# Reading 32-bit matmul operands from two places in turns: a hybrid DeltaNet and block-attention layer on one Trainium2 core

## The chip, the core and the metric

The kernel runs on one core of a Trainium2 chip. A core has five engines that run side by side and meet at semaphores: TensorE (PE) for matmuls, ScalarE (ACT) and VectorE (DVE) for elementwise work, GpSimd (POOL), and SyncE (SP), which here issues the transfers from memory. TensorE holds one operand of a matmul in its array (the stationary one, brought there by a weight load) and streams the other one through it column by column (the moving one). Matmul results go to PSUM, which has eight banks; all else lies in SBUF.

The metric is device time in microseconds (us) of one execution, and of several runs the median is taken.

## What is computed

One decoder layer for 256 tokens of width 1024. A normalised and modulated input goes through one wide projection. Its columns feed a gated DeltaNet branch (4 heads of 128, chunks of 64 tokens) and a block attention branch (8 heads of 64); both come back to width 1024, are gated and summed, go through an output projection, and are added to the input.

```python
h = rms_norm(x, g_pre) * (1 + scale[:, None, :]) + shift[:, None, :]
qkv_dn, z_dn, beta_logit, a_logit, qkv_mb, z_mb, merge_logit = jnp.split(h @ w_in, cuts, axis=-1)
qkv_dn = jax.nn.silu(causal_depthwise_conv(qkv_dn, conv_w))
o_dn = gated_delta_rule_chunked(l2_normalize(q_dn), l2_normalize(k_dn), v_dn, g, beta)
o_dn = rms_norm(o_dn.transpose(0, 2, 1, 3), dn_norm_g) * jax.nn.silu(z_dn...)
y_dn = o_dn.reshape(b, s, DN_WIDTH) @ w_proj_dn
o_mb = moba_attention(q_mb, k_mb, v_mb)[:, :, :s]
y_mb = (o_mb.transpose(0, 2, 1, 3).reshape(b, s, MB_WIDTH) * jax.nn.silu(z_mb)) @ w_proj_mb
gate_dn, gate_mb = jnp.split(jax.nn.sigmoid(merge_logit), N_BRANCH, axis=-1)
mixed = (gate_dn * y_dn + gate_mb * y_mb) @ w_out
return x + gate[:, None, :] * rms_norm(mixed, g_post)
```

With 256 tokens there is one attention block, so the attention is plain causal attention over 256 keys.

## The kernel before

All tensors are float32. A large product is made of three matmuls in the type float32r, a rounded 32-bit form that goes through TensorE in one pass: each operand is split into a rounded part `hi` and a rest `lo`, and hi·hi, lo·hi and hi·lo are summed in PSUM. For a weight this split is one ACT instruction (`CAST whi<-raw`) and one DVE instruction (`wlo<-raw,whi`) for each 512 KB tile (`split`). Small products, with plain float32 operands, take four passes, and the trace has two records for each of them. Transposes are also done by TensorE.

The stages, with the names that the trace shows:

- **start, x**: x is loaded, its row norms are computed, and 16 float32 matmuls with a diagonal matrix transpose and scale it into `xT`.
- **first** (`ada`, `h_ops`, `phase1`): eight steps k. Each loads two 512 KB tiles of the modulation weights (`wss`), which DVE reduces, and two of the input weights (`raw`); ACT and DVE make `hhi[k]` and `hlo[k]` from `xT`; then 48 float32r matmuls of 256 columns add into eight PSUM banks. Weights are stationary there, `hhi` and `hlo` are moving.
- **conv, norm, decay, gram, subst, quad, rec**: the DeltaNet chain, mostly short DVE steps and small float32 matmuls, ending in a square root over `so`, the normalised output `AT<-bank_d,so`, eight transposes (`bank_d<-pr,AT`) and the split of the result into `obh`, `obl` (`o_out`).
- **att**: scores, softmax and values of four pairs of heads; results in `obh`, `obl` too.
- **gemm**: 16 jobs, the other columns of the wide projection. Fifteen have 48 float32r matmuls of 256 columns; job 6 (`gemm_v`) has 48 of 264 columns. In jobs 6 and 7 `hhi` and `hlo` are stationary and the weights are moving. They have no hurry, so they stand between the small steps of the two branches as work for TensorE.
- **proj, out, tail**: 8 times 24 float32r matmuls of 256 columns from `obh`, `obl` (8 weight tiles `in_wpj`), and the output projection, in each of 8 steps 3 x 3 matmuls of 512 and 3 x 2 of 256 columns (8 weight tiles `in_wo`); then the final norm and the store.

The order on each engine is decided at build time by `Machine.schedule`. Every call through `T`, `A`, `V`, `G` or `DQ` only records an instruction; each instruction has a price (`price`) and a rank (the longest priced path behind it), to which `BOOST`, a table of numbers by stage, is added. A list scheduler then picks, engine by engine, the ready instruction with the highest sum. On the chip the order on each engine is fixed. An engine that waits for one instruction holds up all that is queued behind it.

Weight tiles go through four `raw` buffers and five pairs `whi`, `wlo`. A load waits until its buffer has been split.

Of the kernel before, what the change touches and what calls it, by code (L numbers as in the profile page):

```python
# [11 lines left out]
AF = mybir.ActivationFunctionType  # L12
# [5 lines left out]
P = 128  # L18
D = 1024
S = 256  # L20
KT = D // P
# [16 lines left out]
class Machine:  # L38
# [13 lines left out]
    BOOST = dict(ada=55100, ada0=3000, ada1=308600, ada3=55200, ada4=-3500, ada5=20900, ada6=-74400, ada7=700, att=300, att0=-800100, att1=-391600, att2=19200, att3=1407600, att4=400, att5=-159100, att6=200900, att7=660900, beta=-4000, conv=635700, conv0=-1113500, conv1=-582700, conv2=-1729900, conv3=198400, conv4=-4800, cut=-634400, cut0=-28600, cut1=162000, cut2=42100, cut5=919400, cut7=-1900, decay=-251800, decay0=4600, decay1=669500, fin0=105600, fin1=-600, first=203500, first0=159700, first2=100, first3=-65100, first4=-89800, first5=105500, first7=-179600, gate=277800, gate0=4300, gate1=38200, gate2=-4400, gate3=13300, gate4=-400, gate5=-48600, gate6=-58900, gate7=284300, gemm=-7900, gemm1=-198800, gemm10=82200, gemm11=535900, gemm12=98200, gemm13=-227200, gemm14=1222400, gemm15=1316400, gemm2=47400, gemm4=61900, gemm5=-847400, gemm6=352100, gemm7=47500, gemm8=-3200, gemm9=-796900, gram=85700, gram0=-275200, gram1=-154600, mod=2100, mod0=-111400, mod1=18700, mod2=-53700, mod3=76700, mod4=-388200, mod5=-7800, mod6=92400, mod7=5500, norm=-269600, norm0=31000, norm1=-11700, norm3=-18200, norm4=80100, norm5=-250700, out0=-818300, out0_0=-46700, out0_1=33900, out0_2=-17900, out0_3=8800, out0_4=1385300, out0_5=27400, out1=-900, out1_0=-6500, out1_2=-16500, out1_3=200, out1_4=-30400, out1_5=-2249400, out1_6=73500, out1_7=4300, prep=-15700, proj=599600, proj1=-200, proj2=-69200, proj3=-361300, proj4=538400, proj5=-6400, proj6=-640500, proj7=-785200, quad=354400, rec=2016500, rest=-200900, start=-187700, subst=100, tail=83100, x=-116200)  # L52
# [71 lines left out]
    def price(part, method, out, ins, args, kw):  # L124
# [123 lines left out]
def block_kernel(ctx: ExitStack, tc: tile.TileContext, I, out):  # L248
# [39 lines left out]

    def tok(t):
        return slice(t * P, (t + 1) * P)  # L290
# [127 lines left out]
    def h_ops(k):  # L418
        hf = mem([P, S], f"hf{k}", tag="cv")
        for h in (hhi[k], hf):  # L420
            A.activation(h, xT[:, k] if k else xb[0][:, 0:S], AF.Identity, bias=ab[:, k, 0:1], scale=ab[:, k, 1:2])
        V.tensor_sub(hlo[k], hf, hhi[k])


    def phase1(k, parts):
        for j in range(16):
# [36 lines left out]
    szd = mem([P, H, S], "szd")  # L463
# [11 lines left out]
    def ev_silu(dst):  # L475
        return lambda b: silus.append(A.activation(dst, v2(b), AF.Silu))

    jobs = [ev_silu(szd[:, 0:2]), ev_silu(szd[:, 2:4]), ev_silu(szm[:, 0:2]), ev_silu(szm[:, 2:4])]
# [13 lines left out]
    lg = mem([P, 2, NT, H], "lg")  # L492

    def gemm_v():

        bs = [bank("g", f"v{t}") for t in range(NT)]
        for k0, k1 in ((0, 3), (3, 6), (6, 8)):
# [4 lines left out]
            for t in range(NT):  # L502
                for k in range(k0, k1):
                    o, c = bs[t][:, 0:VW], slice((k - k0) * VW, (k - k0 + 1) * VW)
                    op = mm(o, hhi[k][:, tok(t)], whi[:, c], k == 0, False)
                    mm(o, hlo[k][:, tok(t)], whi[:, c], False, False)
                    last = mm(o, hhi[k][:, tok(t)], wlo[:, c], False, k == KT - 1)
                    M.behind(op, order[-1:])
                    order.append(last)
        for t in range(NT):  # L510
            V.tensor_copy(lg[:, :, t], bs[t][:, 256:VW].rearrange("p (n h) -> p n h", n=2))
            A.copy(mv[:, t, 0:256], bs[t][:, 0:256])

    def gemm(i):
        b = bank("g", f"g{i}")
        for j in range(2):
            whi, wlo = split(raw("w2", 2 * i + j - 2 * (i > 6)), f"w2{i}{j}")
            for k in range(KT):
                if i == 7:
# [3 lines left out]
                    op = mm(o, h, whi[:, c], kk == 0 and t == 0, False)  # L523
                    mm(o, l, whi[:, c], False, False)
                    last = mm(o, h, wlo[:, c], False, kk == KT - 1)
                else:
                    o = b[:, j * S : (j + 1) * S]
                    op = mm(o, whi[:, tok(k)], hhi[k], j == 0 and k == 0, False)
                    mm(o, whi[:, tok(k)], hlo[k], False, False)
                    last = mm(o, wlo[:, tok(k)], hhi[k], False, k == KT - 1)  # L530
# [41 lines left out]
    M.stage("prep")  # L572

# [52 lines left out]
    def scores(pair):  # L626
# [11 lines left out]
        for h, s_ in banks_.items():  # L638
# [5 lines left out]
            for t, c in cut:  # L644
                ex_ = A.activation(e[:, c], sms[:, c], AF.Exp, bias=mx[:, h, t : t + 1], scale=SCALE, accum_out=rs[:, h, t : t + 1])
# [7 lines left out]
    def values(pair):  # L653
# [21 lines left out]
        A.copy(obh[:, 1, pair], obm)  # L675
        V.tensor_sub(obl[:, 1, pair], obm, obh[:, 1, pair])
# [191 lines left out]
    def o_out(po, t):  # L868
# [196 lines left out]
```

## Time and profile before

| | us |
|---|---|
| median of 3 runs (lowest to highest) | 239.1 (238.16 to 240.05) |
| the profiled execution, its own time | 238.06 |
| its span, from first to last instruction | 236.2 |
| mean granted TensorE clock | 0.988 of full speed |

The profile gives busy time by engine. A matmul's record lasts longer than the distance to the next matmul's start, since matmuls are pipelined; so a busy TensorE says that it has work, and the distance between starts says at what rate it works. The chain of waits follows the work back from the last instruction: a row such as "64.66 28.16 PE bank_g L236 x240" is a stretch that begins at 64.66 us, lasts 28.16 us and consists of 240 records on PE that write bank group g, one after the other with no wait. All instructions are issued from one helper line, L236, so groups are told apart by the tiles that they read and write: "bank_g<-hlo,whi" is a matmul with moving operand hlo and stationary operand whi.

### The profile page before, as it was taken

The numbers are of one execution on the slowest core, as the hardware profiler recorded it, in microseconds if no ns is written. First come the engines' busy times: TensorE is split into PE (matmuls) and PEld (weight loads), VectorE is DVE, ScalarE is ACT, GpSimd is POOL, SyncE is SP. The second block draws the span as 40 slices with busy tenths as digits, with TensorE's granted clock in tenths as the row PEclk, the third lists the DMA queues.
The fourth block names the chain that finished last, engine by engine and source line by source line (L and its number), as shares of the span: only waits on it lengthen the run. The fifth ranks groups of instructions, "written<-read, shape, count | busy, mean of one in ns | idle before, by whom it ended". The sixth has DMA issues, their size and how long they took to land.

```text
span 236.2 us, 4934 instructions
## 1 busy us (share of the span) xinstructions
PE 227.2 (96%) x1902; PEld 216.8 (92%) x1902; DVE 194.9 (83%) x440; ACT 142.1 (60%) x281; POOL 1.2 (1%) x7
## 2 busy tenths in 40 slices
PE   8699999999999999999999999999999999999990
PEld 8699999999999999799998999898999999899980
DVE  0879999987999985689998999699888986488663
ACT  6585565558888675997446563663368841365141
POOL 1000000000000000000000000000000000000000
PEclk9799999999999999999999999999999999999998
DMA  7999999985957767411582410897788630584013
GB/s 219 396 416 406 389 400 337 395 294 181 309 183 276 241 198 205 154 21 72 147 297 81 121 71 0 296 338 253 253 268 298 228 123 0 183 280 162 0 60 120
DMA packets 15271, 51.20 MB, mean 217 GB/s; under 512 B 1680, under 2 KB 2064, under 8 KB 15248
## 3 DMA queue, kind: packets, MB, share of 16 engines
q1 hardware_dynamic: 15248, 50.89, 61.5%
q8 instruction: 15, 0.25, 0.4%
q14 instruction: 8, 0.07, 0.1%
HBM read 49.83 MB, written 1.05 MB: 215 GB/s over the span
## 4 chain that ended last, share of the span: by engine, by line
PE 90%; DMA 4%; DVE 2%; ACT 1%; issue 1%; SPq 0%; DVEq 0%; ACTq 0%
PE bank_g L236 51%; PE bank_d L236 24%; PE bank_m L236 15%; DMA x<-in_x 2%; DMA raw<-in_wo 2%; DVE xT L236 1%; ACT L236 1%; DVE vT L236 1%; ACT DT L236 0%; DVE r L236 0%; SPq L236 0%; DVE AT L236 0%; ACT whi L236 0%; DVEq L1061 0%; DVE so L236 0%
## 5 line engine op out<-in xcount | busy, mean ns | idle before, releaser
L236 ACT CAST whi<-raw 128x1024 fp32r<-128x1024 f32 (+2 forms) x68 | 67.2, 996 | 35.0 <-DMA raw<-in_w 14.7
L236 DVE TENSOR_TENSOR wlo<-raw,whi 128x1024 fp32r<-128x1024 f32 (+2 forms) x68 | 77.6, 1158 | 7.9 <-ACT whi L236 7.0
L236 PE MATMUL bank_g<-hlo,whi 128*128 128x256 f32 x256 | 69.2, 284 | 0.0
L236 PE MATMUL bank_g<-hhi,whi 128*128 128x256 f32 x256 | 69.1, 284 | 0.0
L236 PE MATMUL bank_g<-hhi,wlo 128*128 128x256 f32 x256 | 68.9, 282 | 0.0
L236 PEld LDWEIGHTS bank_g<-hhi,whi 128*128 128x128 f32 x256 | 46.6, 188 | 0.7 <-issue 0.5
L236 PEld LDWEIGHTS bank_g<-hlo,whi 128*128 128x128 f32 x256 | 46.7, 188 | 0.6 <-issue 0.5
L236 PEld LDWEIGHTS bank_g<-hhi,wlo 128*128 128x128 f32 x256 | 46.7, 188 | 0.3 <-issue 0.2
L236 PE MATMUL bank_g<-obl,whi 128*128 128x256 f32 x64 | 13.3, 284 | 0.0
L236 PE MATMUL bank_g<-obh,whi 128*128 128x256 f32 x64 | 13.3, 284 | 0.0
L236 PE MATMUL bank_g<-obh,wlo 128*128 128x256 f32 x64 | 13.2, 283 | 0.0
L236 ACT ACTIVATE hhi<-cv 128x256 fp32r<-128x256 f32 x8 | 3.3, 417 | 13.6 <-DVE cv L236 13.6
L236 ACT ACT_TABLE_LOAD x8 | 10.3, 1283 | 1.7 <-DVE cv L236 0.8
L236 PEld LDWEIGHTS bank_g<-obh,whi 128*128 128x128 f32 x64 | 10.3, 191 | 0.5 <-ACT obh L236 0.2
L236 DVE CUSTOM_DVE_ANT_0 wss<-wss,AT,pr 128x1024 f32<-128x1024 f32 x8 | 10.2, 1280 | 0.3 <-DMA wss<-in_wss 0.3
L236 PEld LDWEIGHTS bank_g<-obh,wlo 128*128 128x128 f32 x64 | 10.3, 191 | 0.2
L236 DVE SCALAR_TENSOR_TENSOR tl<-wss,bank_g 128x512 f32<-128x512 f32 x8 | 5.5, 687 | 5.9 <-PE bank_g L236 5.9
L236 DVE CUSTOM_DVE_ANT_0 wss<-wss,AT,b2g 128x1024 f32<-128x1024 f32 (+1 forms) x8 | 10.2, 1276 | 0.0
L236 PEld LDWEIGHTS bank_g<-obl,whi 128*128 128x128 f32 x64 | 10.1, 191 | 0.1
L236 PE MATMUL bank_g<-whi,hhi 128*128 128x264 f32 (+1 forms) x32 | 9.1, 284 | 0.0
L236 PE MATMUL bank_g<-whi,hlo 128*128 128x264 f32 (+1 forms) x32 | 9.1, 284 | 0.0
L236 PE MATMUL bank_g<-wlo,hhi 128*128 128x264 f32 (+1 forms) x32 | 9.1, 283 | 0.0
(223 smaller groups left out, 448.0 us busy)
## 6 DMA issues: line engine op xcount, KB each, us to landing
raw<-in_w SPq DMA_DIRECT2D x43, 512.0 KB, 4.6
wss<-in_wss SPq DMA_DIRECT2D x15, 512.0 KB, 6.6
raw<-in_wg SPq DMA_DIRECT2D x8, 512.0 KB, 4.7
raw<-in_wpj SPq DMA_DIRECT2D x8, 512.0 KB, 4.3
raw<-in_wo SPq DMA_DIRECT2D x8, 512.0 KB, 4.4
raw<-in_w SPq DMA_DIRECT2D x6, 256.0 KB, 7.3
x<-in_x SPq DMA_DIRECT2D x2, 512.0 KB, 4.1
x<-in_x SPq DMA_DIRECT2D x1, 1024.0 KB, 8.0
```

The lines of the kernel that those rows point to most:

```text
L236: o["ins"] = getattr(self.engines[o["part"]], o["method"])(*o["args"], **o["kw"])
```

## The change

The moving operand of every large float32r matmul is laid out differently, and read in another order.

- **Layout.** Each group of 32 columns of such an operand lies "woven": first the 16 even columns, then the 16 odd ones. The matmul's access pattern (`mmw`) reads from the two halves in turns, so the columns reach the array in their natural order, while the addresses alternate between two places 16 elements apart. Results are written straight to PSUM. For `gemm_v` the whole 264 columns lie as two halves of 132.
- **Who makes the layout.** The weights that are moving (`wo`, `w2[12:14]`, `wv`) are reordered on the host. On the chip, instructions that wrote the operand anyway now read with a stride of two: the copies from PSUM into `xT`, the first `h_ops`, the exponentials of the softmax, the casts and subtractions for `obh`, `obl`.
- **What follows from it.** Where `hhi` and `hlo` are stationary, tokens now come out in woven order; for the values this agrees with the woven softmax, and for the decay logits one `STREAM_SHUFFLE` over 16 columns puts the tokens back. In `o_out` the factor `gd` moves from the DVE multiply into the ACT cast and the DVE subtraction. `szd` has another order of its dimensions.
- **The planner.** The price of a float32r matmul is now `n / 2.4 + 5` ns, the assumed rate of transfers 400 instead of 360, and the table `BOOST` has new numbers throughout.

No matmul, no weight split and no byte of transfer is added or taken away.

```diff
-    BOOST = dict(ada=55100, ada0=3000, ada1=308600,
...
+    BOOST = dict(ada=33200, ada0=-46900, ada1=119400, ada2=-90900,
...
-            held = n * 4 * list(out.ap)[0][1] / 360.0
+            held = n * 4 * list(out.ap)[0][1] / 400.0
...
-                return max(n * 0.4531 + 4, 111.0) - 6 * (list(out.ap)[0][1] < P), 60.0
+                return n / 2.4 + 5, 60.0
...
+    def woven(ap):
+        return ap.rearrange("p (q b a) -> p q a b", b=16, a=2)
+    def lies(ap):
+        return ap.rearrange("p (q a b) -> p q a b", b=16, a=2)
+    def mmw(o, l, r, first, last=True):
+        q = dict(a=2, b=16)
+        return mm(o.rearrange("p (q b a) -> p q b a", **q), l, r.rearrange("p (q a b) -> p q b a", **q), first, last)
...
-    A.copy(xT[:, 1], xb[0][:, S : 2 * S])
+    A.copy(lies(xT[:, 1]), woven(xb[0][:, S : 2 * S]))
     for q in range(1, 4):
-        A.copy(xT[:, 2 * q : 2 * q + 2], v2(xb[q]))
+        A.copy(lies(xT[:, 2 * q : 2 * q + 2].rearrange("p k s -> p (k s)")), woven(xb[q]))
...
-            mm(a, whi[:, c], hhi[k], k == 0 and j % 2 == 0, False)
-            mm(a, whi[:, c], hlo[k], False, False)
-            mm(a, wlo[:, c], hhi[k], False, k == KT - 1)
+            mmw(a, whi[:, c], hhi[k], k == 0 and j % 2 == 0, False)
+            mmw(a, whi[:, c], hlo[k], False, False)
+            mmw(a, wlo[:, c], hhi[k], False, k == KT - 1)
...
+                        rv = r[:, c].rearrange("p (a b) -> p b a", a=2)
+                        last = mm(o.rearrange("p (b a) -> p b a", a=2), l[k][:, tok(t)], rv, k == n == 0, k == KT - 1 and n == 2)
...
-            V.tensor_copy(lg[:, :, t], bs[t][:, 256:VW].rearrange("p (n h) -> p n h", n=2))
+            V.tensor_copy(lgw[:, :, t], bs[t][:, 256:VW].rearrange("p (n h) -> p n h", n=2))
...
+    V.stream_shuffle(lg.rearrange("p n t h -> p (n t h)"), lgw.rearrange("p n t h -> p (n t h)"), [16 * (i % 2) + i // 2 for i in range(32)])
...
-                ex_ = A.activation(e[:, c], sms[:, c], AF.Exp, bias=mx[:, h, t : t + 1], scale=SCALE, accum_out=rs[:, h, t : t + 1])
+                ex_ = A.activation(lies(e[:, c]), woven(sms[:, c]), AF.Exp, bias=mx[:, h, t : t + 1], scale=SCALE, accum_out=rs[:, h, t : t + 1])
...
-        A.copy(obh[:, 1, pair], obm)
-        V.tensor_sub(obl[:, 1, pair], obm, obh[:, 1, pair])
+        A.copy(lies(obh[:, 1, pair]), woven(obm))
+        V.tensor_sub(lies(obl[:, 1, pair]), woven(obm), lies(obh[:, 1, pair]))
...
-        V.scalar_tensor_tensor(ob, v4(pt), pr[:, PSI_GD : PSI_GD + 1], szd[:, :, tok(t)], op0=mul, op1=mul)
-        A.copy(obh[:, 0, :, tok(t)], ob)
-        V.tensor_sub(obl[:, 0, :, tok(t)], ob, obh[:, 0, :, tok(t)])
+        gd = pr[:, PSI_GD : PSI_GD + 1]
+        V.tensor_tensor(lies(ob.rearrange("p h c -> p (h c)")), woven(pt), woven(szd[:, t]), mul)
+        A.activation(obh[:, 0, :, tok(t)], ob, AF.Copy, scale=gd)
+        V.scalar_tensor_tensor(obl[:, 0, :, tok(t)], ob, gd, obh[:, 0, :, tok(t)], op0=mul, op1=sub)
...
+    lie = lambda a: a.reshape(*a.shape[:-1], -1, 16, 2).swapaxes(-1, -2).reshape(a.shape)
+    wo = lie(wo)
+    w2[12:14] = lie(w2[12:14])
+    wv = wv.reshape(P, KT, VW // 2, 2).swapaxes(2, 3).reshape(P, KT * VW)
```

The other calls of `mm` in `gemm`, `out_mm` and `proj` become `mmw` in the same way.

The new table moves instructions on every engine. Two places matter below, both at the end of the DeltaNet chain. The first is ACT around the square root over `so`. Before, it stands there behind the cast of a weight tile (`whi_118<-raw_79`, the first tile of `in_wo`):

```order
L236 ACTIVATE jk_140,so_161<-bank_d_67 128x128
L236 ACTIVATE jk_139,so_161<-bank_d_67 128x128
L236 ACTIVATE wss_75<-bank_g_63 128x512
L236 CAST whi_122<-raw_78 128x1024
L236 ACTIVATE jk_140,so_161<-bank_d_66 128x128
L236 ACTIVATE jk_139,so_161<-bank_d_66 128x128
L236 ACTIVATE jk_140,so_161<-bank_d_66 128x128
L236 ACTIVATE jk_139,so_161<-bank_d_66 128x128
L236 CAST whi_118<-raw_79 128x1024
L236 ACT_TABLE_LOAD
L236 ACTIVATE so_161<-so_161 128x8
L236 ACT_TABLE_LOAD
```

In the changed kernel the same place on ACT has two exponentials of the attention (`pex`) ahead of the square root:

```order
L236 CAST obh_143<-obm_150 128x256
L236 ACTIVATE jk_141,so_162<-bank_d_66 128x128
L236 ACTIVATE jk_140,so_162<-bank_d_66 128x128
L236 ACTIVATE jk_141,so_162<-bank_d_66 128x128
L236 ACTIVATE jk_140,so_162<-bank_d_66 128x128
L236 ACTIVATE pex_89,rs_145<-sms_148,mx_146 128x256
L236 ACTIVATE pex_89,rs_145<-sms_148,mx_146 128x128
L236 ACT_TABLE_LOAD
L236 ACTIVATE so_162<-so_162 128x8
L236 ACT_TABLE_LOAD
L236 ACTIVATE pex_90,rs_145<-sms_149,mx_146 128x256
```

Both casts, of the first `in_wpj` and the first `in_wo` tile, now stand behind the square root, and the attention's last pairs stand where they were.

The second place is PE around the eight transposes (`bank_d<-pr_71,AT_86`) that this square root leads to. Before:

```order
L236 MATMUL bank_g_63<-hhi_0_99,whi_120 128x256
L236 MATMUL bank_g_63<-hlo_0_107,whi_120 128x256
L236 MATMUL bank_g_63<-hhi_0_99,wlo_125 128x256
L236 MATMUL bank_d_65<-pr_71,AT_86 128x128 x4
L236 MATMUL bank_d_67<-pr_71,AT_86 128x128 x4
L236 MATMUL bank_g_63<-hhi_0_100,whi_120 128x256
L236 MATMUL bank_g_63<-hlo_0_108,whi_120 128x256
```

In the changed kernel:

```order
L236 MATMUL bank_g_64<-hhi_0_98,wlo_123 128x256
L236 MATMUL bank_m_69<-pr_71,pex_91 128x128 x3
L236 MATMUL bank_m_70<-pr_71,pex_92 128x128 x3
L236 MATMUL bank_d_65<-pr_71,AT_86 128x128 x4
L236 MATMUL bank_g_64<-hhi_0_99,whi_119 128x256
L236 MATMUL bank_d_67<-pr_71,AT_86 128x128 x4
L236 MATMUL bank_m_69<-pr_71,pex_89 128x128 x3
L236 MATMUL bank_m_70<-pr_71,pex_90 128x128 x3
L236 MATMUL bank_m_68<-sms_147,mv_88 64x256
```

The transposes come earlier among the matmuls of the gemm jobs: 30 of these were left behind them, now 57, and the transposes of two attention pairs stand beside them.

## Rows read from the trace of the kernel before

**Rows 1.** The page's first part: engine, busy us (share of span), instructions.
```profile
PE 227.2 (96%) x1902; PEld 216.8 (92%) x1902; DVE 194.9 (83%) x440; ACT 142.1 (60%) x281; POOL 1.2 (1%) x7
```

**Rows 2.** The span in 40 slices of 5.9 us: granted clock, transfer rate.
```profile
PEclk9799999999999999999999999999999999999998
...
GB/s 219 396 416 406 389 400 337 395 294 181 309 183 276 241 198 205 154 21 72 147 297 81 121 71 0 296 338 253 253 268 298 228 123 0 183 280 162 0 60 120
```

**Rows 3.** The chain of waits: start us, length us, engine, bank, records.
```profile
22.17 0.70 PE bank_d L236 x6
...
57.51 5.63 PE bank_g L236 x46
...
64.66 28.16 PE bank_g L236 x240
...
221.94 6.30 PE bank_d L236 x27
```

**Rows 4.** The chain of waits, small float32 matmuls (gram; state and output).
```profile
123.26 0.86 PE bank_d L236 x4
...
165.42 1.78 PE bank_d L236 x16
```

**Rows 5.** Timeline of PE from 100 us, first and 36th matmul (none missing between).
```profile
99.80 0.28 PE L236 MATMUL bank_g<-hhi,whi 128*128 128x256 f32 x1
...
103.95 0.28 PE L236 MATMUL bank_g<-hhi,wlo 128*128 128x256 f32 x1
```

**Rows 6.** Groups of PE by shape: names, shape, count | busy us, mean ns.
```profile
L236 PE MATMUL bank_g<-hlo,whi 128*128 128x256 f32 x256 | 69.2, 284 | 0.0
...
L236 PE MATMUL bank_g<-obl,whi 128*128 128x256 f32 x64 | 13.3, 284 | 0.0
...
L236 PE MATMUL bank_d<-whi,hlo 128*128 128x512 f32 x24 | 9.0, 396 | 0.0
L236 PE MATMUL bank_m<-hhi,whi 128*128 128x256 f32 x48 | 9.0, 280 | 0.0
...
L236 PE MATMUL bank_g<-whi,hlo 128*128 128x264 f32 x16 | 4.6, 285 | 0.0
...
L236 PE MATMUL bank_d<-xT 128*128 128x256 f32 x16 | 4.1, 379 | 0.0
```

**Rows 7.** Groups of weight loads (PEld) by shape.
```profile
L236 PEld LDWEIGHTS bank_g<-hhi,whi 128*128 128x128 f32 x256 | 46.6, 188 | 0.7 <-issue 0.5
...
L236 PEld LDWEIGHTS bank_d<-vs,ktok 128*128 128x128 f32 x8 | 1.0, 191 | 0.0
```

**Rows 8.** Busy us by engine in stretches of 10 us: PE, PEld, DVE, ACT, POOL.
```profile
30.00:40.00 10.00, 10.00 (x88) 10.00 (x87) 10.00 (x14) 5.94 (x9) 0.00 (x0) 1.00 0.99 360
...
60.00:70.00 10.00, 10.00 (x86) 10.00 (x85) 9.97 (x23) 8.64 (x15) 0.00 (x0) 1.00 0.70 236
...
130.00:140.00 10.00, 10.00 (x87) 10.00 (x86) 9.82 (x61) 5.82 (x12) 0.00 (x0) 1.00 0.34 111
```

**Rows 9.** Timeline at the end of the DeltaNet chain: ACT, then PE.
```profile
172.46 1.05 ACT L236 CAST whi<-raw 128x1024 fp32r<-128x1024 f32 x1 [3.59 <-DMA raw<-in_wpj]
...
175.16 1.05 ACT L236 CAST whi<-raw 128x1024 fp32r<-128x1024 f32 x1 [0.61 <-DMA raw<-in_wo]
...
177.52 0.21 ACT L236 ACTIVATE so<-so 128x8 f32<-128x8 f32 x1
...
178.95 1.25 PE L236 MATMUL bank_d<-pr,AT 128*128 128x128 f32 x8 [0.19 <-DVE AT L236]
```

**Rows 10.** Groups of DVE and ACT by shape, nearest to the touched instructions.
```profile
L236 DVE SCALAR_TENSOR_TENSOR bt<-bank_d,pr,szd 128x512 f32<-128x512 f32 x2 | 1.5, 751 | 0.3 <-PE bank_d L236 0.2
...
L236 DVE TENSOR_TENSOR obl<-bt,obh 128x512 fp32r<-128x512 f32 x2 | 1.4, 684 | 0.0
...
L236 DVE STREAM_SHUFFLE cv<-jk 128x88 f32<-128x88 f32 x1 | 0.3, 252 | 0.0
...
L236 ACT ACTIVATE pex<-sms,mx 128x256 f32<-128x256 f32 x8 | 4.0, 506 | 2.2 <-DVE mx L236 2.2
```

More of the change, by code (lines that the diff above doesn't have):

```diff
@@ L420, in h_ops @@
         for h in (hhi[k], hf):
-            A.activation(h, xT[:, k] if k else xb[0][:, 0:S], AF.Identity, bias=ab[:, k, 0:1], scale=ab[:, k, 1:2])
+            A.activation(lies(h), lies(xT[:, k]) if k else woven(xb[0][:, 0:S]), AF.Identity, bias=ab[:, k, 0:1], scale=ab[:, k, 1:2])
         V.tensor_sub(hlo[k], hf, hhi[k])
@@ L462, in block_kernel @@
     mv = mem([P, NT, 512], "mv", tag="mv")
-    szd = mem([P, H, S], "szd")
+    szd = mem([P, NT, H * P], "szd")
     szm = mem([P, H, S], "szm")
@@ L492, in block_kernel @@
     lg = mem([P, 2, NT, H], "lg")
+    lgw = mem([P, 2, NT, H], "lgw")
     def gemm_v():
@@ L504, in gemm_v @@
                     o, c = bs[t][:, 0:VW], slice((k - k0) * VW, (k - k0 + 1) * VW)
-                    op = mm(o, hhi[k][:, tok(t)], whi[:, c], k == 0, False)
-                    mm(o, hlo[k][:, tok(t)], whi[:, c], False, False)
-                    last = mm(o, hhi[k][:, tok(t)], wlo[:, c], False, k == KT - 1)
+                    turns = [(hhi, whi), (hlo, whi), (hhi, wlo)]
+                    for n, (l, r) in enumerate(turns):
+                        rv = r[:, c].rearrange("p (a b) -> p b a", a=2)
+                        last = mm(o.rearrange("p (b a) -> p b a", a=2), l[k][:, tok(t)], rv, k == n == 0, k == KT - 1 and n == 2)
+                        op = op if n else last
                     M.behind(op, order[-1:])
@@ L522, in gemm @@
                     o, h, l = b[:, t * 256 : (t + 1) * 256], hhi[kk][:, tok(t)], hlo[kk][:, tok(t)]
-                    op = mm(o, h, whi[:, c], kk == 0 and t == 0, False)
-                    mm(o, l, whi[:, c], False, False)
-                    last = mm(o, h, wlo[:, c], False, kk == KT - 1)
+                    op = mmw(o, h, whi[:, c], kk == 0 and t == 0, False)
+                    mmw(o, l, whi[:, c], False, False)
+                    last = mmw(o, h, wlo[:, c], False, kk == KT - 1)
                 else:
                     o = b[:, j * S : (j + 1) * S]
-                    op = mm(o, whi[:, tok(k)], hhi[k], j == 0 and k == 0, False)
-                    mm(o, whi[:, tok(k)], hlo[k], False, False)
-                    last = mm(o, wlo[:, tok(k)], hhi[k], False, k == KT - 1)
+                    op = mmw(o, whi[:, tok(k)], hhi[k], j == 0 and k == 0, False)
+                    mmw(o, whi[:, tok(k)], hlo[k], False, False)
+                    last = mmw(o, wlo[:, tok(k)], hhi[k], False, k == KT - 1)
                 M.behind(op, order[-1:])
@@ L935, in out_mm @@
         o = outs[n][:, 0 : c1 - c0]
-        mm(o, mh[m][:, tok(t)], whi[:, c0:c1], m == 0, False)
-        mm(o, ml[m][:, tok(t)], whi[:, c0:c1], False, False)
-        mm(o, mh[m][:, tok(t)], wlo[:, c0:c1], False, m == 7)
+        mmw(o, mh[m][:, tok(t)], whi[:, c0:c1], m == 0, False)
+        mmw(o, ml[m][:, tok(t)], whi[:, c0:c1], False, False)
+        mmw(o, mh[m][:, tok(t)], wlo[:, c0:c1], False, m == 7)
         M.stage(*last)
@@ L950, in block_kernel @@
                 c = tok(4 * br + k)
-                mm(o, phi[:, c], obh[:, br, k], br == 0 and k == 0, False)
-                mm(o, phi[:, c], obl[:, br, k], False, False)
-                mm(o, plo[:, c], obh[:, br, k], False, k == 3)
+                mmw(o, phi[:, c], obh[:, br, k], br == 0 and k == 0, False)
+                mmw(o, phi[:, c], obl[:, br, k], False, False)
+                mmw(o, plo[:, c], obh[:, br, k], False, k == 3)
         mt = mem([P, 2, S], f"mt{m}", tag="tl")
```

7 lines of the change are left out of this document (4 added, 3 removed).

## The prediction

> **What bounds the kernel now.** I read the page's engine table first. TensorE is busy for 227.2 of 236.2 us, DVE for 194.9, ACT for 142.1 [rows 1]; the reader is to see that nothing but PE can be the first bound, and that DVE is the next. The transfer row says that memory is pressed only in the first 50 us, at about 400 GB/s [rows 2]. The chain of waits agrees: from 57.5 to 92.8 us, for instance, it is nearly all matmuls without a gap between them [rows 3]. But busy is not the rate, so the second thing to read is the distance between starts.
>
> A float32r matmul of 256 columns takes 28.16 / 240 = 117.3 ns in that stretch, and 0.70 / 6 = 117 in the first stage [rows 3]; from 100 us on it is (103.95 - 99.80) / 35 = 118.6 [rows 5]. One of 264 columns takes 5.63 / 46 = 122.4, one of 512 columns 6.30 / 27 = 233.3 [rows 3]. Twice the columns cost twice the time, so this is a cost by column, not by instruction: 0.456 ns. [...]
>
> Is it lost in the array or on the way to it? The plain float32 matmuls answer this. Each has two records. Those of gram stream 256 columns twice in a record, 512 column steps, and take 0.86 / 4 = 215 ns [rows 4, 6], 0.42 ns a step. [...]
>
> **The change, part by part.**
>
> *Reading in turns.* From the code, 1344 matmuls of 256 columns are affected (384 in the first stage, 720 in gemm, 192 in proj, 48 in out), 48 of 264 and 72 of 512; the trace has them in groups of x256, x64, x48, x24 and x16, one of each three shown or named by size [rows 6]. No row shows a strided moving operand, so I bound the new distance. [...] From above, if it helps at all: 117.3. For a value between I take the nearest row: state and output matmuls, 16 records of 256 column steps in 1.78 us, 111.3 ns each [rows 4]. Each of these also has its own 128-column weight load, 191 ns long where the float32r one has 188 [rows 7], so this row answers a second question: overlapping weight loads can follow each other every 111 ns. I take 111.3 for 256 columns, 114.6 for 264 (eight columns more at 0.417) and 216 for 512 (the 215 of gram, rounded up). The gain:
>
> - first stage, 384 x (117.3 - 111.3) = 2.3 us
> - gemm up to 93 us, 240 x 6.0 = 1.4 us
> - the other 480 of gemm, 192 of proj and 48 of out, 720 x (118.6 - 111.3) = 5.3 us
> - 48 x (122.4 - 114.6) = 0.4 us, and 72 x (233.3 - 216) = 1.2 us
>
> Together 10.6 us. [...]
>
> [...] Reading in turns makes each access go to another place. [...]
>
> *Strided reads elsewhere.* On ACT four copies into xT, the first two h_ops, 16 exponentials and four casts read with stride two, on DVE four subtractions and two multiplies. Near rows of these shapes take 0.4 to 0.7 us [rows 10]. Lower bound nothing, upper bound each doubled: about 12 us on ACT, which is idle for 94 of 236 us [rows 1], and 3 us on DVE. I take nothing; ACT's idle time hides it, and without that cover only the xT copies and h_ops lie on the path at the start, some 0.6 us.
>
> *Small edits.* The STREAM_SHUFFLE costs at most 0.25 us of DVE (a row of 88 elements takes that [rows 10], this one has 16), while PE works on gemm. In o_out a DVE scalar_tensor_tensor of 751 ns and a subtraction of 684 [rows 10] change places in kind; nothing is added. The host's reordering is not in the time.
>
> *The new order.* Before, the chain's square root waits on ACT behind the cast of the first in_wo tile: the cast starts at 175.16 when its transfer lands, the root follows at 177.52, and PE reaches the transposes at 178.95 with 0.19 us of waiting [rows 9]. So the DeltaNet chain ended just in time. With faster matmuls PE would be there about 7 us earlier (2.3 + 0.4 + 1.4 + most of 5.3) and would wait, had the order stayed. In the new order that root stands ahead of both casts, one of which waited 3.59 us for its transfer [rows 9], and 57 instead of 30 gemm matmuls are left behind the transposes. What stands behind the root now, the in_wpj casts, is needed only for proj, and the 57 matmuls, 57 x 0.111 = 6.3 us, cover them. On SP the second load of x and the two row loads change places among the last weight loads; bytes stay the same.
>
> *What it gives back.* In the first stage a step needs 2.1 MB, 5.2 us at 400 GB/s [rows 2], and PE would need 48 x 111.3 = 5.3: the margin is gone, and DVE is busy there for all of 10 us [rows 8]. From 57 to 180 us DVE stands at up to 9.97 and 9.82 of 10 [rows 8], so in the fullest stretches PE will now wait for a wlo or a small step. I set 0.5 us for the first stage and 1 us for the rest, an estimate: about 7 us must come out of a stretch in which DVE has a tenth to spare.
>
> **The sum.** 238.06 (the profiled execution) - 10.6 + 1.5 = 229.0 us. The median before lies 1.0 above the profiled execution; for the median after I add half of that: **229.5 us**. From the bounds of the terms its own range is 224.5 to 232.5: 108.4 ns per matmul (106.7 and the 1.7 that gram's 215 has over 213.3) would gain about 14 us; twice the waiting and 113 ns give the upper end.
>
> **The rivals.**
>
> - *Others become the bound.* The matmuls get faster, but DVE (83% busy [rows 1], 100% in places [rows 8]) or the transfers of the first stage set the pace, and half the gain or more comes back as PE waiting. For it: those full stretches. Against it: PE now waits for almost nothing, and the new order moves the one chain that was just in time. 238.06 - 10.6 + 6 = 233.5, up to 235.5.
> - *Changing place costs.* A fetch pays for going to another place in memory, and the present loss is this cost, paid rarely. [...] It decides as soon as the new distance is over 119 ns. For it: something by column is lost on the way from memory. [...]
> - *It does nothing.* The loss has to do with the type, not with the addresses; 117 to 119 ns stay. Then only the order changes, with a chain that ends earlier but no idle time to win: PE waits for little now. 237 to 240, 238.5.
>
> **How the numbers follow.** Forecast 0.60, others become the bound 0.18, nothing 0.10, changing place costs 0.12. The range for 8 in 10 takes the first two whole and the edge of the third: 224.5 to 236.5. About 1% is what a measurement of this kernel can tell from no change, so faster means below 236.7: 0.60 + 0.18 = 0.78; within 1%: 0.10; slower: 0.12.
>
> **What would show it.** In the timeline of gemm, starts 111 ns apart (117 to 119: nothing; over 119: the second rival), in out 216 apart for 512 columns, and the 264-column ones near 115. If 512 columns take 216 but 256 stay at 117, weight loads were the limit after all. In the stretch table, DVE at 9.9 of 10 over several stretches and new waits of PE for DVE or a transfer: the first rival. At the end of the chain, the root on ACT should follow its DVE step at once, and PE should reach the transposes without a wait. The prediction is wrong if the distance is not between 108 and 114, or if PE waits for more than some 4 us in all between 57 us and the end.

## The result, and the profile of the changed kernel

The changed kernel takes 235.91 us (median of 4, 235.15 to 236.04); the kernel before took 239.49 beside it. The ratio is 0.985, with a 95% interval of 0.980 to 0.990: 3.5 us faster, where 9.6 were forecast. The profiled execution took 236.04 us, its span is 234.3; that is 1.9 us less than the profiled span before (236.2), so the trace explains somewhat less than the medians show.

The page of the changed kernel, span and engine table (for [rows 1]):

```profile
span 234.3 us, 4925 instructions
PE 221.3 (94%) x1902; PEld 209.0 (89%) x1902; DVE 195.9 (84%) x442; ACT 142.4 (61%) x281; POOL 1.2 (1%) x7
```

TensorE's busy time fell by 5.9 us, from 227.2. The forecast gain was 10.6. Its idle time, span less busy, rose from 9.0 to 13.0 us. So there are two things to explain: 4.7 us of gain missing inside the busy time, and 4 us of new idle time (10.6 - 4.7 - 4.0 leaves the 1.9 between the spans).

The distance of the matmuls is not the reason. The timeline of PE in gemm (start, duration; for [rows 5]), the first and last of an unbroken run of 166 records, and the chain of waits (start, length; for [rows 3]):

```profile
123.01 0.28 PE L236 MATMUL bank_g<-hhi,whi 128*128 128x256 f32 x1
...
141.44 0.28 PE L236 MATMUL bank_g<-hhi,whi 128*128 128x256 f32 x1
```

```profile
76.27 10.62 PE bank_g L236 x95
...
199.38 3.67 PE bank_d L236 x17
```

(141.44 - 123.01) / 165 = 111.7 ns, 10.62 / 95 = 111.8, and 216 for 512 columns. Forecast were 111.3 and 216. The share of PE in the chain fell from 90% to 50% all the same. PE's waits by releaser (total, times, longest) show more small ones than before, where `pex`, `ones` and one of 0.2 us for `AT` were all:

```profile
PE bank_d L236 <- DVE pex L236: 2.2, 1, 2.2
PE bank_g L236 <- ACT whi L236: 1.0, 1, 1.0
PE bank_m L236 <- POOL ones L236: 1.0, 1, 1.0
PE bank_g L236 <- DVE tl L236: 1.0, 1, 1.0
PE bank_g L236 <- DVE lgw L236: 0.6, 1, 0.6
...
```

Together the list has 7.1 us of waits, before 3.2. No new wait is long. A record lasts 0.28 us while the next starts 0.11 us later, so a wait of up to 0.17 us hides within busy time.

### The profile page after: what moved, and what is told of

Read it like the earlier page. It is cut to its first block, busy times and chain, and to the rows that moved or that the text cites. A ratio compares the mean times of both kernels' runs of the same rounds, so it can differ in the third digit from the quotient of the medians.

```text
span 234.3 us, 4925 instructions
## 1 busy us (share of the span) xinstructions
PE 221.3 (94%) x1902; PEld 209.0 (89%) x1902; DVE 195.9 (84%) x442; ACT 142.4 (61%) x281; POOL 1.2 (1%) x7
## 4 chain that ended last, share of the span: by engine, by line
PE 50%; DMA 20%; DVE 14%; ACT 10%; issue 3%; SPq 1%; DVEq 0%; ACTq 0%
PE bank_g L236 32%; PE bank_d L236 14%; DMA raw<-in_w 10%; DMA wss<-in_wss 5%; PE bank_m L236 5%; DVE wlo L236 4%; ACT whi L236 3%; DVE wss L236 2%; ACT L236 2%; DMA raw<-in_wpj 2%; ACT jk L236 2%; DVE xT L236 2%; DMA raw<-in_wv 2%; DVE vT L236 1%; SPq L236 1%
## 5 line engine op out<-in xcount | busy, mean ns | idle before, releaser
L236 PE MATMUL bank_g<-hhi,wlo 128*128 128x256 f32 x256 | 67.5, 277 | 0.0
L236 PE MATMUL bank_g<-hlo,whi 128*128 128x256 f32 x256 | 67.4, 277 | 0.0
L236 PEld LDWEIGHTS bank_g<-hhi,whi 128*128 128x128 f32 x256 | 47.5, 192 | 2.1 <-DVE lgw L236 0.8
L236 PEld LDWEIGHTS bank_g<-hhi,wlo 128*128 128x128 f32 x256 | 47.5, 192 | 0.4 <-issue 0.3
L236 PEld LDWEIGHTS bank_g<-hlo,whi 128*128 128x128 f32 x256 | 47.3, 192 | 0.4 <-issue 0.2
L236 PE MATMUL bank_g<-obh,wlo 128*128 128x256 f32 x64 | 12.5, 275 | 0.0
L236 PE MATMUL bank_g<-obl,whi 128*128 128x256 f32 x64 | 12.4, 275 | 0.0
L236 DVE CUSTOM_DVE_ANT_0 wss<-wss,AT,pr 128x1024 f32<-128x1024 f32 x8 | 10.2, 1281 | 2.1 <-DMA wss<-in_wss 2.1
L236 DVE CUSTOM_DVE_ANT_0 wss<-wss,AT,b2g 128x1024 f32<-128x1024 f32 (+1 forms) x8 | 10.2, 1274 | 0.0
L236 PE MATMUL bank_m<-hhi,whi 128*128 128x256 f32 x48 | 9.2, 275 | 0.0
L236 ACT ACTIVATE pex<-sms,mx 128x256 f32<-128x256 f32 (+1 forms) x16 | 7.5, 480 | 2.6 <-DVE mx L236 2.5
L236 DVE SCALAR_TENSOR_TENSOR vT<-raw,sc,vT 128x1024 f32<-128x1024 f32 x7 | 8.9, 1275 | 0.0
```

Of the source, the lines that this page charges most:

```text
L236: o["ins"] = getattr(self.engines[o["part"]], o["method"])(*o["args"], **o["kw"])
```

## Experiments

### Reads and order, each alone

The change has two halves: the woven reads, and a new order (the table and two prices). Each was put into the kernel without the other.

```diff
 weave_old_order: the changed kernel, with the table and prices of before
-    BOOST = dict(ada=33200, ada0=-46900, ...
+    BOOST = dict(ada=55100, ada0=3000, ...
-            held = n * 4 * list(out.ap)[0][1] / 400.0
+            held = n * 4 * list(out.ap)[0][1] / 360.0
-                return n / 2.4 + 5, 60.0
+                return max(n * 0.4531 + 4, 111.0) - 6 * (list(out.ap)[0][1] < P), 60.0
 plain_new_order: the kernel before, with the opposite lines
```

> The woven reads alone: every layout edit of the change, but the planner's table, its price for float32r and its transfer rate as before, so that the order on each engine is that of the kernel before (with the one added shuffle). Theory 'order': the matmuls start every 111 to 112 ns as in the changed kernel (10 us less work for TensorE), and what was given back was given back by the new order, above all by the late split that held up four loads at 41 to 45.5 us; then this kernel is faster than the changed one, 228 to 233 us. Theory 'other engines': transfers, VectorE and ScalarE set the pace whatever the order, and give back about 7 us here too: 234 to 237 us. In an order planned for slower matmuls the DeltaNet chain should then show waits of PE before the eight transposes.

> The new order alone: the kernel before with the new table, price and transfer rate, and plain reads. Theory 'order': distances of 117 to 119 ns stay and the new order costs something by itself, 241 to 247 us. Theory 'other engines': the order costs nothing, 238 to 241 us, since PE is the bound and hides its waits.

| | order of before | new order |
|---|---|---|
| plain reads | 238.65 | 244.0, ratio 1.024 (1.021 to 1.027) |
| reads in turns | 232.2, ratio 0.972 (0.969 to 0.974) | 235.9, ratio 0.985 (0.980 to 0.990) |

The reads gain 6.5 us in the old order and 8 in the new one; the new order costs 5.4 us with plain reads and 3.7 with woven ones. The changed kernel's own time was taken apart from the other three, beside a kernel before of 239.49 instead of 238.65 us. The ratios allow for that: by them the reads gain 9 us in the new order, and the new order costs 3.2 us with woven reads. weave_old_order is faster than both kernels. Run again beside later experiments it took 232.78 (ratio 0.973, 0.968 to 0.977):

> The same kernel as weave_old_order (woven reads, order of before) once more, on the chip of the next two runs, for a direct comparison: 232.2 us again, 231 to 233 by every theory.

The first suspect in the new order was the first stage, where one split stands later and four loads are issued 4 us later. front_old orders the stages up to `first` as before and the rest as in the changed kernel.

```diff
 front_old, the second line in words
+    FRONT = ("start", "x", "ada", "mod", "cut", "first", "rest")
+    key[n] = time in the old order if stage in FRONT else time in the new one
```

> The changed kernel, with the first stage (norms, modulation, splits, its 384 matmuls, its loads) in the order of the kernel before, and all later work in the new order. Theory 'late split in the first stage': the four loads are issued near 41 us again, the matmuls of 264 columns end near 62 instead of 64.8 us, and the whole is 2 to 4 us faster than the changed kernel, 232 to 234 us. Theory 'other engines': the first stage ends when its transfers do, and nothing changes, 235 to 237 us.

It took 235.11 us (ratio 0.985, 0.983 to 0.987), no change. The loads went out early again (from 40.84 us, in the changed kernel from 45.54), and the time was lost a little later, in `gemm_v`, where PE now waits 1.6 us for a `wlo`. So the suspect falls: moving one stage moves the wait.

### DVE's pace, or the order itself?

To tell a late DVE from a bad order, the order of each kernel was written out as a list and kept, and only the length of DVE's splits was cut.

```diff
 light_after, light_old, light_before: each kernel in its own order
+            if turn["wlo"] > 5:
+                cs = slice(c * n, c * n + 64)
             V.tensor_sub(lo[:, cs], t[:, cs], hi[:, cs])
 half_load_after: the changed kernel in its own order
+            m = n // 2 if turn["raw"] > 8 else n
-            load(t[:, c * n : (c + 1) * n], src[:, c * n : (c + 1) * n])
+            load(t[:, c * n : c * n + m], src[:, c * n : c * n + m])
```

> The changed kernel with its own order of instructions on every engine, but from the sixth low part on DVE subtracts only 64 of 1024 columns (the other columns keep what an earlier tile left, so low parts are left out of the result). A split of 1.22 us on DVE becomes about 0.2; some 50 us of DVE's 196 fall away. Theory A, DVE's pace: TensorE waits in the changed kernel because splits and conv steps on DVE come late; with DVE relieved most of what was given back returns, 229 to 231 us. Theory B, transfers: the waits come from tiles that land late; DVE frees its tiles about 1 us earlier, so 1 to 2 us return, 234 to 235. Theory C, the order itself: steps stand in the wrong sequence in the queues of ACT and SP whatever their length; 235 to 236.

> The same relief of DVE (64 of 1024 columns subtracted from the sixth low part on, the low parts left out) in the kernel with the woven reads and the order of before, which took 232.2 us. Forecast gain of the faster matmuls: 10.6 us, measured 6.5. Theory A, DVE's pace: the missing 4 us come back, 228 to 229.5 us. Theory B, transfers: about 231 to 232. Theory C, the order: unchanged, 232.

> Control: the same relief of DVE in the kernel before (low parts left out from the sixth on). Its TensorE waited for nothing for more than 0.2 us after the start. All theories: unchanged within 1%, 237.5 to 239.5. A gain of more than 2 us would mean that TensorE's distance of 117 to 119 ns hides short waits for DVE, and then part of the forecast gain was never TensorE's own.

> The changed kernel with its own order, but from the ninth weight tile on only half of the columns is loaded (the other half keeps what an earlier tile left, so the result uses wrong weights there). Each such transfer moves 0.26 instead of 0.52 MB; about 55 tiles, some 14 MB of 51 fall away. Theory A, DVE's pace: 235 to 236. Theory B, transfers: tiles land 0.6 us or more earlier, 2 to 4 us return, 231 to 234. Theory C, the order: 235 to 236.

| | us | ratio (95%) |
|---|---|---|
| light_before | 237.98 | 0.998 (0.994 to 1.002) |
| light_old | 228.31 | 0.957 (0.954 to 0.959) |
| light_after | 233.69 | 0.979 (0.977 to 0.982) |
| half_load_after | 234.61 | 0.982 (0.979 to 0.985) |

The control is what it had to be: with plain reads DVE's length changes nothing. With the order of before and light splits the woven reads gain 237.98 - 228.31 = 9.7 us; the forecast's terms with the measured distances (111.7, 112.6, 216) make 10.2. The gain of the reads is all there as soon as the splits are short. With splits at full length 4 us of it are lost.

In the new order short splits return only 2.2 us, and half the transfers 1.3; by the ratios it is 1.4 and 0.7, with intervals that overlap with the changed kernel's, so neither is large and the second is not clear of noise. Engine tables of light_old and light_after:

```profile
PE 216.2 (96%) x1902; PEld 207.3 (92%) x1902; DVE 139.0 (61%) x442; ACT 141.9 (63%) x281; POOL 1.2 (1%) x7
```

```profile
PE 219.9 (95%) x1902; PEld 207.9 (90%) x1902; DVE 138.9 (60%) x442; ACT 141.3 (61%) x281; POOL 1.2 (1%) x7
```

The same 1902 records keep PE busy for 3.7 us longer in the new order, and idle for 2.0 us longer (the spans are 226.2 and 231.9). Since short waits hide in busy time, this alone doesn't say whose time it is; it makes a cost on TensorE itself worth testing.

How the 4 us are lost in the order of before is seen best around job 6, in the timeline of weave_old_order (rows of several engines; in brackets the idle time ahead of an instruction and what ended it):

```profile
54.77 2.49 DVE L236 TENSOR_TENSOR wlo<-raw,whi 128x792 fp32r<-128x792 f32 x3 [1.08 <-ACT whi L236]
...
55.78 0.33 SPq L236 DMA_DIRECT2D raw<-in_w  x1
...
62.69 1.04 ACT L236 CAST whi<-raw 128x1024 fp32r<-128x1024 f32 x1 [1.18 <-DMA raw<-in_w]
63.64 0.64 ACT L236 COPY mv<-bank_g 128x256 f32<-128x256 f32 x2
...
64.06 0.38 PE L236 MATMUL bank_g<-hhi,whi 128*128 128x256 f32 x1 [1.26 <-ACT mv L236]
```

Read it from the bottom. PE waits 1.26 us for a bank that ACT empties (`mv`). ACT stood at a cast that waited 1.18 us for its tile. By the order of the tiles that is the load of 55.78, which went out as DVE finished the first of three splits (54.77; they take 0.98, 0.98 and 0.70 us) and so freed a buffer; two more followed it in 1.5 us, and it landed late among them. The list names ACT, but the wait goes back to splits on DVE. In light_old the same splits take 0.23 us each, from 53.78 on, the loads go out from 54.03, and the two ACT instructions find nothing to wait for:

```profile
59.85 1.03 ACT L239 CAST whi<-raw 128x1024 fp32r<-128x1024 f32 x1
...
60.78 0.64 ACT L239 COPY mv<-bank_g 128x256 f32<-128x256 f32 x2
```

PE's wait is gone there. It is 1.3 of the 4 us, and not a fixed part: in the profile of weave_again PE waits 0.4 us at this place and more at others. The 240 matmuls behind it show the gain of the reads in both kernels (chain of waits of weave_old_order, then of light_old, to be held against 28.16 us in [rows 3]):

```profile
64.06 27.07 PE bank_g L236 x240
```

```profile
61.81 26.81 PE bank_g L239 x240
```

### What the new order costs on TensorE

The scores and values of attention are matmuls of 64 rows or 64 columns, four to a group. The new order cuts some groups: other matmuls stand between their members. paired_after puts three groups together again and moves nothing else but four DVE steps that depend on it.

```diff
 order on PE, paired_after against the changed kernel
-MATMUL bank_m2_70<-sms_1_148,mv_0_88 64x256
 MATMUL bank_m1_69<-mk_0_131,mq_0_130 128x128
 MATMUL bank_m0_68<-mk_0_131,mq_0_130 128x256
 MATMUL bank_m1_69<-mk_0_131,mq_0_130 128x256
+MATMUL bank_m2_70<-sms_1_148,mv_0_88 64x256
 ...
```

> The changed kernel with ten matmuls of attention moved on TensorE, nothing else but four steps of DVE that had to follow: the four scores of head pairs 2 and 3, which the new order cuts into 1 + 3 and 3 + 1, and the four value products of pair 2, cut into 1 + 3, stand together again. In the trace of the changed kernel each cut of such a group costs about 0.3 us of TensorE beside the matmuls' own time (4 together end 0.2 us late, 1 + 3 end 0.3 + 0.3 to 0.4 late). Theory A, the new order costs TensorE time of its own by cutting groups of 64-row matmuls: 1.0 to 1.4 us faster, 234.5. Theory B, the order costs only by late splits and transfers: 235.9, or slower, since the softmax of pair 3 starts 1 us later.

It took 234.55 us (ratio 0.982, 0.979 to 0.985). That is 1.35 us less, as expected, though the intervals of the two ratios overlap and by the ratios it is 0.7. The timelines of PE settle the place. The same eight matmuls (16 records), from the first to the next one that follows, in the changed kernel and in paired_after:

```profile
156.69 0.49 PE L236 MATMUL bank_m<-mk,mq 64*128 64x128 f32 x2
157.11 0.65 PE L236 MATMUL bank_m<-sms,mv 128*64 128x256 f32 x2
157.68 0.92 PE L236 MATMUL bank_m<-mk,mq 64*128 64x128 f32 x6
158.53 0.86 PE L236 MATMUL bank_m<-sms,mv 128*64 128x256 f32 x6
159.33 0.38 PE L236 MATMUL bank_g<-hhi,whi 128*128 128x256 f32 x1
```

```profile
157.48 0.93 PE L239 MATMUL bank_m<-mk,mq 64*128 64x128 f32 x8
158.34 0.87 PE L239 MATMUL bank_m<-sms,mv 128*64 128x256 f32 x8
159.14 0.38 PE L239 MATMUL bank_g<-hhi,whi 128*128 128x256 f32 x1
```

2.64 us against 1.66: two cuts cost 0.98 us, with no wait in either. PE's busy time fell from 221.3 to 219.9.

light_paired has both edits, the short splits and the groups together.

> The changed kernel's order with DVE relieved as in light_after (233.7 us; low parts from the sixth on are left out) and the attention groups of pairs 2 and 3 put together as in paired_after. If the cut groups are a cost of TensorE's own, it adds up: 233.7 - 1.3 = 232.4, still 4 us over the order of before with the same relief (228.3). If they only cost because DVE is late beside them: 233.7.

It took 231.43 us (ratio 0.970, 0.965 to 0.974), 2.3 less than light_after, where 1.3 were expected; the cost adds up, so it is TensorE's own. Against light_old 3.1 us of the new order's 5.4 are left, and no experiment takes them apart.

The traces of light_old and light_after say where the 5.7 us between their spans lie. PE's distances from each start to the next, summed by kind of matmul, are longer in the new order by 1.2 us in scores and values, 1.2 in the other small float32 matmuls, 0.8 in the transposes of `pex`, 1.3 in proj, and 1.2 among the float32r matmuls of the first stage and gemm. Most of proj's share is one wait (light_after):

```profile
184.40 0.33 SPq L239 DMA_DIRECT2D raw<-in_wpj  x1
...
189.42 1.04 ACT L239 CAST whi<-raw 128x1024 fp32r<-128x1024 f32 x1 [3.11 <-DVE cv L239]
...
190.52 0.38 PE L239 MATMUL bank_g<-obh,whi 128*128 128x256 f32 x1 [0.74 <-ACT whi L239]
```

The list names DVE, but the last part of the load that went out at 184.40 landed at 189.32, just ahead of the cast. In light_old the same load, the fourth of `in_wpj`, goes out at 176.48, and PE has no such wait.

The order of before cuts groups too, those of pairs 0 and 1. paired_old joins them, and the values of pair 1.

```diff
 order on PE, paired_old against weave_old_order
-MATMUL bank_m1_69<-mk_0_131,mq_0_130 128x128
-MATMUL bank_m2_70<-mk_0_131,mq_0_130 128x128
 ...
+MATMUL bank_m2_70<-mk_0_131,mq_0_130 128x128
 ...
+MATMUL bank_m1_69<-mk_0_131,mq_0_130 128x128
```

> The kernel with woven reads and the order of before (232.2 us) with the scores of head pairs 0 and 1, which that order cuts into pieces of 2, 2, 1 and 3, and the values of pair 1, cut into 3 + 1, put together on TensorE. Theory A (cut groups cost about 0.3 us each): 1.2 to 1.5 us faster, 230.8. Theory B (TensorE loses only where it waits for others): 232 to 233.

It took 234.35 us (ratio 0.980, 0.976 to 0.984): no gain, if anything a loss, against the 230.8 expected. Its executions went from 232.43 to 235.94 us, and the profile is of the fastest. Its engine table and two of PE's waits say where the gain went there:

```profile
PE 216.3 (94%) x1902; PEld 206.6 (90%) x1902; DVE 194.4 (84%) x442; ACT 142.3 (62%) x281; POOL 1.2 (1%) x7
```

```profile
PE bank_d L239 <- DVE AT L239: 2.0, 1, 2.0
PE bank_d L239 <- DVE r L239: 1.3, 1, 1.3
```

Both waits were 0.4 us in weave_old_order. PE's busy time is 216.3 us where weave_old_order had 219.0, but that fall is not all gain, since waits that hid in busy time became listed ones. What the groups themselves cost is the sum of PE's distances over the stretches of scores and values, from the first start of a stretch to the next other matmul:

| | stretches | us |
|---|---|---|
| weave_old_order, groups cut | 11 | 8.02 |
| paired_old | 8 | 6.81 |
| changed kernel, groups cut | 13 | 9.25 |
| paired_after | 10 | 7.65 |

So joining saves 1.2 us on TensorE here, as expected. But TensorE is early, the DeltaNet chain isn't, and most of it comes back before the transposes. Why the median lies another 1.9 us above the profiled execution is not shown. The table also says how much of the difference between the two orders is cut groups: 9.25 - 8.02 = 1.2 us, since the old order cuts some as well.

### Relieving DVE without leaving work out

Short splits leave work out. Three kernels tried to move DVE's work instead, in the order of weave_old_order or, for best, of paired_old. scale_on_act also joins the values of pair 1 on TensorE.

```diff
 pool_old
+            E = G if name[:2] == "w2" and name[2:-1] in ("2", "3", "4", "5", "7", "8", "10", ...) else V
-            V.tensor_sub(lo[:, cs], t[:, cs], hi[:, cs])
+            E.tensor_sub(lo[:, cs], t[:, cs], hi[:, cs])
 best: pool_old in the order of paired_old
 scale_on_act
-                V.tensor_scalar_mul(e[:, c], e[:, c], rs[:, h, t : t + 1])
+                A.activation(e[:, c], e[:, c], AF.Copy, scale=rs[:, h, t : t + 1])
```

> The kernel with woven reads and the order of before (232.2 us), with 22 of the subtractions that make low parts (gemm jobs 2 to 5, 7, 8, 10 to 12, 14 and 15) on GpSimd, which is idle, in place of DVE: 27 us of DVE's 194 fall away, all of them where the low part is needed only 5 us or more later. With DVE relieved everywhere the kernel took 228.3. Theory A, DVE's pace is what holds the faster matmuls back between 65 and 160 us: 229.5 to 231. Rival: GpSimd takes several times as long as DVE for 1024 columns, or slows DVE by reading beside it; then tiles are freed later and TensorE waits more: 232 to 237.

> Both edits of the two runs above together: woven reads, order of before, attention groups of pairs 0, 1 and the values of pair 1 put together, 22 subtractions on GpSimd. If both theories hold their gains add up: 232.2 - 1.4 - 2 = about 229. If GpSimd is too slow: as that run, less 1.4.

> Woven reads, order of before, but the 16 multiplications that divide the softmax by its sums (0.28 and 0.34 us each on DVE, 5 us together) run on ACT in the same places, where a row of this shape takes about 0.45 us, 7 us together; the values of head pair 1 stand together on TensorE. Theory A, what holds this kernel back from 95 us on is DVE, by way of the DeltaNet chain that ends before the eight transposes: 0.5 to 1.5 us faster than weave_again, 231. Rival, ACT's queue is as full there (casts that wait for transfers): same or slower, 232 to 234.

pool_old took 246.79 us and best 246.99 (both 1.032, 1.029 to 1.036), 14 us slower than weave_old_order: the rival. A row of GpSimd and two of DVE in pool_old, by form:

```profile
L239 POOL TENSOR_TENSOR wlo<-raw,whi 128x1024 fp32r<-128x1024 f32 x22 | 52.9, 2415 | 109.7 <-ACT whi L239 109.5
```

```profile
L239 DVE TENSOR_SCALAR pex<-pex,rs 128x256 f32<-128x256 f32 x8 | 4.9, 616 | 0.0
...
L239 DVE TENSOR_TENSOR tm<-cv,X 128x32 f32<-128x32 f32 x1 | 2.4, 2401 | 0.0
```

GpSimd needs 2.42 us for what takes DVE 1.22, and some DVE steps beside it stretch: 2.40 us for one that takes 0.19 in weave_old_order, about the length of one GpSimd instruction, and 2.50 for one of the eight `pex` (the others take 0.35). Many of the steps that stretch are the DeltaNet chain. TensorE waits for that chain (4.6 us for `vT`, 3.6 for `r`), and the mean granted clock is 0.968 where weave_old_order had 0.991. How much of the 14 us goes with that clock is not shown.

scale_on_act took 232.80 us beside weave_again's 232.78, though its joined values alone save 0.4 us of TensorE: the 16 multiplications, 5 us of DVE, were not what TensorE waits for. No kernel that computes everything was faster than weave_old_order.

### The reads by themselves

In this kernel the gemm jobs, all but 6 and 7, read their 256 columns in various sequences; one of them, job 13, reads the same column 256 times.

```diff
+    TURNS = {1: (2, 16), 2: (2, 8), 3: (2, 4), 4: (2, 2), 5: (2, 32), 8: (2, 128), 10: (4, 8), 14: (2, 64)}
+    STEPS = {9: 2, 11: 4}
```

> The changed kernel, in which the gemm jobs read the same 256 moving columns in other orders (data and layout as they are, so these jobs compute something else): job 0, 12 plain; 1 and 15 in turns 16 elements apart; 2, 3, 4 in turns 8, 4, 2 apart; 5, 14, 8 in turns 32, 64, 128 apart; 9 with a stride of 2 and 11 with a stride of 4 within 32 columns; 10 in turns from four places 8 apart; 13 the same column 256 times. Distances between starts: if what costs is staying in one small piece of memory, then turns at 16 elements or more give 111 to 112 ns, plain 117, turns within 2 or 4 elements 117, strides in between; if any alternation does, all turns give 111. [...]

What it measured stands in the last section. The total, 249.8 us, says nothing beside that.

## Why the prediction was wrong, point by point

- **Distance: right.** 111.7 ns against 111.3 for 256 columns, 112.6 against 114.6 for 264 (5.18 us for 46 in the chain of weave_old_order), 216 against 216 for 512. The argument from gram held: its records of 256 columns, two to a matmul, take 215 ns each [rows 4], as long as 512 float32r columns in turns (216), so 0.42 ns a step, where float32r took 0.456 with plain reads; the author put the difference down to the fetch. The same column 256 times, which leaves the fetch nothing to move on to, also takes 112 (last section). No run shows the 0.417 ns a column that the forecast uses for 264 columns, or the 106.7 and 213.3 ns in its range; the runs showed 0.42 ns a column at 512 columns, and 111.7 ns for 256. The 4 ns by which 256 columns exceed half of 216 stay in turns and with the same column, so they aren't a matter of which columns are read.
- **Weight loads: right.** They follow each other every 112 ns, as the row had it. Whether they are the bound at that distance is open: eight more columns, 264 for 256, cost 0.9 ns, where 0.42 ns a column would make 3.4.
- **Changing place costs, It does nothing: both fell.** The price decided at 119 ns, and turns are faster than 117: 111.7. Which reads do take longer than plain ones is shown in the last section.
- **What it gives back: the term that was mis-sized.** 1.5 us were set; about 7 came. The reason given, that DVE has a tenth to spare, was the right place to look: with full splits 4 us are lost even in the old order, and none to speak of with short ones. The estimate read DVE's busy share of long stretches. What counts is a late split, as at job 6: it holds a `raw` buffer, so a load, so a cast on ACT, and with it all that is queued behind that cast. (The upper end of the range was also summed a little low: 113 ns and twice the waiting give about 233, not 232.5.)
- **The new order: the step that failed.** It was taken as needed and as free. Both were wrong. "With faster matmuls PE would be there about 7 us earlier and would wait, had the order stayed": the order stayed in weave_old_order, and PE waited 0.4 us there (1.0 in weave_again). The steps of the DeltaNet chain wait for matmuls themselves, so they came earlier too. The clearest case is light_old, with the whole gain and DVE relieved: the transposes start 6.5 us earlier than before (178.95 in [rows 9]), after a wait of 0.5.

```profile
172.49 1.25 PE L239 MATMUL bank_d<-pr,AT 128*128 128x128 f32 x8 [0.46 <-DVE AT L239]
```

With DVE not relieved the chain does set a limit (2.0 us of waiting in paired_old), but not one of 7 us. And the new order was priced only by the waits it removes. It cost 3.2 to 3.7 us (5.4 with short splits): shown are cut groups, 1.2 us more than in the old order, which the order on PE could have told ahead of the run, and with short splits 0.7 us of waiting for a later weight load in proj. The rest is spread over small float32 matmuls and short waits, and its cause stays open.

- **Others become the bound: nearest in size (233.5, up to 235.5), right in half its reason.** DVE sets back 4 us in the old order; half the transfers return at most 1.3 in the new one. The measured time lies inside the range, up to 236.5, only through the part that was added for rivals. The forecast gave it 0.18 because "the new order moves the one chain that was just in time", which was the argument that failed.
- **Strided reads elsewhere, small edits: nothing, as forecast.** In weave_old_order, where the order is that of before, ACT is busy for 142.5 us, before 142.1; DVE for 194.3, before 194.9.

## What to carry to other kernels

When one engine's work gets faster and every other engine keeps its pace, size what is given back from the buffers that couple them, not from busy shares: follow one late step through buffer, load and queue to the engine that waits. A new order is a change of its own, with costs of its own on the fast engine, and is to be priced and tested apart from the edit that it comes with; here the old order with the new reads is the best kernel. Attention's matmuls of 64 rows or 64 columns were cheaper here side by side, in groups that nothing cut (by 1.2 and 1.6 us of TensorE); the kernel gets no faster by it where the other engines don't keep up, as paired_old shows (234.35 us against 232.2).

## What the runs showed of the hardware

Float32r matmuls of 256 columns at a granted clock of 1.00, timeline of PE in the kernel patterns. In order: one after the other; in turns, 4 columns apart; in turns, 2 apart; from four places, 8 columns apart; every second column, then the others; the same column 256 times:

```profile
66.82 0.28 PE L236 MATMUL bank_g<-hhi,wlo 128*128 128x256 f32 x1
...
67.52 0.28 PE L236 MATMUL bank_g<-hhi,wlo 128*128 128x256 f32 x1
...
82.75 0.28 PE L236 MATMUL bank_g<-hlo,whi 128*128 128x256 f32 x1
...
83.53 0.28 PE L236 MATMUL bank_g<-hhi,wlo 128*128 128x256 f32 x1
...
88.32 0.29 PE L236 MATMUL bank_g<-hlo,whi 128*128 128x256 f32 x1
...
88.80 0.28 PE L236 MATMUL bank_g<-hhi,wlo 128*128 128x256 f32 x1
...
125.84 0.41 PE L236 MATMUL bank_g<-hhi,whi 128*128 128x256 f32 x1
...
127.20 0.41 PE L236 MATMUL bank_g<-hhi,whi 128*128 128x256 f32 x1
...
132.79 0.30 PE L236 MATMUL bank_g<-hhi,whi 128*128 128x256 f32 x1
...
133.61 0.30 PE L236 MATMUL bank_g<-hhi,whi 128*128 128x256 f32 x1
...
156.99 0.27 PE L236 MATMUL bank_g<-hhi,whi 128*128 128x256 f32 x1
...
158.11 0.28 PE L236 MATMUL bank_g<-hlo,whi 128*128 128x256 f32 x1
```

The rows stand in order of time, so every second column (from 125.84) comes before four places (from 132.79). Six distances in 0.70 us make 117 ns in order; seven in 0.78 make 111 in turns 4 columns apart, and 8, 16, 32, 64 and 128 columns apart gave the same; four in 0.48 make 120 in turns 2 apart, which is no better than in order. Six in 1.36 make 227 for every second column, and six in 0.82 make 137 from four places. Every fourth column took 240 (six in 1.44). The same column 256 times took 112 (ten in 1.12), as in turns.

So two places help at 4 columns' distance, 16 bytes, and at every larger one tried (111 ns against 117), and not at 2 columns (120). Staying at one place is not what costs: the same column over and over is as fast as turns (112). Nor is it a change of place at each read: that costs nothing here when two places 4 or more columns apart take turns and each moves on column by column. Walking in steps of 4 columns doubles the time (240 against 117), and steps of 2 columns come close to it (227). Two sequences are better than one, and four are worse (111, 117 and 137). Why is not shown.
